# Ten of the modulation's tiles in attention instead of twelve, and begun 75 ticks after its start instead of 10

## The chip, the cores and the metric

The kernel runs on one core of a Trainium2 chip. The metric is the device time of one execution in microseconds, lower is better; it is given as the median over several executions. The engines are named as the profile names them: PE is TensorE (matmuls; PEld its weight loads), DVE is VectorE, ACT is ScalarE, POOL is GpSimd, and SP is SyncE, which here mostly issues DMAs.

## The reference

A step of a small diffusion backbone with two layers, width 1024, for 512 latent tokens and 128 context tokens. The first layer's mixer is a bidirectional scan (SSD), the second's is differential attention with 8 heads; each is followed by a gated convolutional network (ConvGLU) with a hidden width of 2816. Every sub-layer is normalised, shifted and scaled, and added back with a gate; shift, scale and gate come from a modulation of the conditioning vectors.

```python
def modulation(cvec, w, b):
    m = jax.nn.silu(cvec) @ w + b          # w: 1024 x 6144 for each layer
    return jnp.split(m[:, None, :], 6, axis=-1)
...
    def one_block(qi):                     # differential attention, 128 queries at a time
        s = jnp.einsum('bqhcd,bkhcd->bhcqk', qi, k, preferred_element_type=F32) * DA_SCALE
        p = jax.nn.softmax(s, axis=-1)
        w = p[:, :, 0] - lam * p[:, :, 1]
        return jnp.einsum('bhqk,bkhd->bqhd', w.astype(v.dtype), v)
...
    for i in range(DEPTH):
        p_sh1, p_sc1, p_g1, p_sh2, p_sc2, p_g2 = modulation(c_ctx[None], mod_w[i], mod_b[i])
        s_sh1, s_sc1, s_g1, s_sh2, s_sc2, s_g2 = modulation(c, mod_w[i], mod_b[i])
        ...
        xp = xp + p_g1 * op
        xs = xs + s_g1 * os_
        xp = xp + p_g2 * conv_ffn(modulate(xp, norm_ffn_g[i], p_sh2, p_sc2), *ffn_p)
        xs = xs + s_g2 * conv_ffn(modulate(xs, norm_ffn_g[i], s_sh2, s_sc2), *ffn_p)
```

The change concerns `modulation` of the second layer: 6144 outputs for two conditioning vectors, each output a dot product over 1024 numbers.

## The kernel before

All activations lie transposed, 128 channels on the partitions and 640 tokens (512 latent, 128 context) in the free dimension; the width of 1024 is eight such tiles. A matrix product in fp32 is made of three matmuls of a split into a rounded high part and a rest (`whi`, `wlo` for weights, `h10h`, `h10l` and the like for activations), so each weight tile is loaded by SP (`raw`, or `raw_15523` with its running number), rounded on ACT (`whi<-raw`) and subtracted on DVE (`wlo<-raw,whi`). The stages follow each other: SSD, the first network (ffn0), attention, the second network (ffn1).

*The modulation of layer 1* is done on DVE, beside other stages. `mod_rest` goes over tiles t0 to t1 − 1 of 48. A tile `mw` is 128 outputs by 1024 weights, 512 KB, loaded by SP (L683) into one of two buffers, one tile ahead. For each of the two conditioning vectors `cb[c]` one DVE instruction multiplies and sums it (L690; the profile calls it CUSTOM_DVE_ANT_0, the order below ISA) into a column of `mod`. The first writes its products into a scratch tile `junk`, the second over `mw`, so that the buffer is free after it; each is followed by a short read of the accumulator. These are "the dots": two for each tile. After eight tiles the bias is added (`mod<-mod,modb`).

*What sets the order.* Side work is written as generators. `self.add(gen, wait)` starts one after `wait` ticks; a tick is a call of `hook()`, which the matrix products make once for each step over k. A `yield n` lets n ticks pass, and in attention `self.gap` is 6, so a tile of two dots takes 12 ticks. `self.drain(t)` runs the rest of a generator at once. Every dot is also held behind the matmul that was recorded last (`self.hold`). A scheduler then makes one fixed order for each engine from what was recorded, and moves other instructions around.

*Which tiles go where* stands in `DOTS`: tiles 0 to 3 at the end of SSD, then up to `DOTS[1]` in ffn0 (beside its up projections and its four calls of `project_out`, the down projection of a part of the hidden channels), the next up to `DOTS[2]` in ffn0's `project_last`, the next up to `DOTS[3]` in attention, and the last eight in ffn1.

*Attention.* `heads` records eight heads in a loop. A head has three dense products from the queue of `next_tile` (q, k, v; 24 ticks together, but none in head 0, whose products are done ahead by `start_tiles`), the rotation of q and k on DVE (`ru`, `q`, `k`, `rope`), and `att_head`: for each of four blocks of 128 queries two score tiles `sl` (one for each map; `sp` for the context's own), their maximum over the row on DVE (L1351, `sm<-sl`), the exponential on ACT (`e<-sl`, L103), the difference of the two maps on DVE (`w<-e,sm,e`), its transposition on PE (`wt`) with copies `wTh` on ACT and `wTl` on DVE, and the product with v (`ov`). The tail of a head normalises its output (`ms` on PE, the `rs_` steps on DVE, and a broadcast: by DMAs to `rsd` and back into `rbc` for heads 0 to 6, by PE into `obc` for head 7). `vout` and `kout` are outputs, `k<-in_ck` the cached keys.

After the loop come the splits of the first six heads' outputs (`o0` to `o5`), the rest of the dots (`self.drain(dots)`), the closing of the pool that holds `mw` (`self.modctx.close()`), and `self.restore()`, which loads the eight tiles of the residual stream `xr_15354` to `xr_15361` from DRAM (L139) into the space of that pool. Then the output projection of the first six heads is recorded (`project_out`, `po<-o0h,whi` and so on, with `xr<-po,mod,xr` on DVE as the gated addition), with head 7 still unfinished, and at last that of heads 6 and 7.

Of the kernel before, what the change touches and what calls it, by code (L numbers as in the profile page):

```python
# [40 lines left out]
RAW = 4  # L41
NS = 4
S0 = 5
DOTS = 4, 24, 28, 40, 48
TH = T // 2
ATT_SPLIT = 6
NF = 11
# [3 lines left out]
class Step:  # L51
# [659 lines left out]
    def ffn(self, l, h, nextnorm, pool):  # L711
# [151 lines left out]
        with self.tc.tile_pool(name=f"sums{l}", bufs=1, side="right", reuse_waits="tile") as tp:  # L863
            self.seven = self.add(operands(sevens, tp), 1)
            for s, (k0, k1) in enumerate(SUB):
                while done < min(k1 + 1, FT):
                    if done == (S0 + 1 if l else 3):
                        junk = lambda: self.slot("sq", "junk", BF16, cols=1024, bufs=1)
                        self.modtask = self.add(self.mod_rest(1, *(DOTS[3:] if l else DOTS[:2]),
                                                              self.cb, self.mod_row, junk), 1)  # L870
# [35 lines left out]
        if not l:  # L906
            self.gap = 3
            junk = lambda: self.slot("t", "junk", BF16, cols=1024, bufs=4)
            more = [self.add(self.mod_rest(1, *DOTS[1:3], self.cb, self.mod_row, junk), 1)]
        self.project_last(mid, range(*SUB[-1]), self.gate(l, 1), nextnorm, parts="CD" if l else "AB", save=not l,  # L910
# [95 lines left out]
    def ssd_group(self, g, xf, Bf, Cf, pool):  # L1006
# [51 lines left out]
        def state(d_, c, pm):  # L1058

            xw = sl("xw", "xw", 512, 2)  # L1060
            self.tt(v3(xw), v3(xt[:, c, :]), self.wst[:, c, heads(d_)].unsqueeze(2).to_broadcast([P, 8, 64]), ALU.mult)
            self.mm(pm, bt[:, c, :], xw, True, True)

        def carry(d_, c, out, pm):

            nh = sl("hs", f"h_{d_}_{c}_", 512, 6)
            if c == NL:
                self.act(nh, pm, AF.Copy)
                nc.sync.dma_start(a["st"][d_, g], nh)
                return  # L1070
            self.tt(v3(nh), v3(hs[d_, c]), self.cd[:, c, heads(d_)].unsqueeze(2).to_broadcast([P, 8, 64]), ALU.mult)
            self.tt(nh, nh, pm, ALU.add)
            hs[d_, out] = nh
# [107 lines left out]
    def ssd(self, h, dtps, nextnorm, pool):  # L1181
# [62 lines left out]
        self.gap, self.rest = 3, 2  # L1244
        early = self.add(self.mod_rest(1, 0, DOTS[0], self.cond_rows(row), row, junk), 4)
        self.project_last(hy, range(8), self.gate(0, 0), nextnorm, save=True, before=[early])
# [201 lines left out]
    def heads(self, h, nextnorm, pool):  # L1448

        nc = self.nc  # L1450
        self.cv = pool.tile([P, D], F32, tag="cv", name="cv", bufs=1)
        nc.sync.dma_start(self.cv, self.a["cv"])
        consts = self.att_consts(pool)
        next(consts)
        o, tk, self.tails, self.held = [], [], {}, {}
        next(consts, None)
        junk = lambda: pool.tile([P, 1024], BF16, tag="junk", name="junk", bufs=1)
        self.gap, self.rest = 6, 0
        dots = self.add(self.mod_rest(1, *DOTS[2:4], self.cb, self.mod_row, junk), 10)
        for hd in range(8):  # L1460
            q, qp = self.att_evac(self.next_tile(h, "q"), hd, "q", pool)
            k, kp = self.att_evac(self.next_tile(h, "k"), hd, "k", pool)
            nc.sync.dma_start(self.a["kout"][hd], kp)
            q = self.att_q(q, hd, pool)
            k = self.att_k(k, hd, pool)
            vs = []
            tk.append(self.add(self.att_head(hd, qp, kp, q, k, vs, o, pool), 1 if hd == 7 else 4))
            self.add(self.att_v(self.next_tile(h, "v"), hd, vs, pool), 1)
            if hd:
                self.drain(tk[hd - 1])  # L1470
        n0 = ATT_SPLIT
        for i in range(n0):
            self.drain(self.tails[i])
        hy = [self.split(o[i], f"o{i}") for i in range(n0)]
        self.drain(dots)
        self.modctx.close()
        self.restore()
        self.project_out(hy, range(n0), self.gate(1, 0), range(KT - 3))
        self.drain(tk[7])
        for t in self.tails.values():  # L1480
            self.drain(t)
        hy += [self.split(o[i], f"o{i}") for i in range(n0, 8)]
        self.project_last(hy, range(n0, 8), self.gate(1, 0), nextnorm, range(8), save=True)
# [200 lines left out]
```

## Time and profile before

| what | value |
|---|---|
| runs of the kernel | 1827.41, 1826.96, 1824.88 us |
| median | 1826.96 us |
| profiled execution, device time | 1828.54 us |
| its span from the first to the last instruction | 1826.8 us, mean PE clock 0.994 |
| ffn0's fourth `project_out` | about 869 to 897 us |
| the heads, from the rows of PE | about 1025 to 1330 us |
| first and last dot in attention | 1044.93 and 1259.49 us |

The profile is one execution. Starts are microseconds from the start of the span. A row of a timeline gives start, duration, engine, line and operation, `out<-in`, and in brackets how long the engine had been idle and what released it. A row of stretches gives window, length, busy time and instructions of PE, PEld, DVE, ACT and POOL, then the clock granted to PE (1.00 is full), the mean busy share of the DMA engines and GB/s. In the rows of one engine alone, only that engine's columns stand.

### The profile page before, as it was taken

Reading aid. Unit: us, or ns where it says so; the run is one execution under the profiler, and the core shown is the slowest. Engines: PE = TensorE matmul, PEld = TensorE weight load, DVE = VectorE, ACT = ScalarE, POOL = GpSimd, SP = SyncE. Lnnn points to the kernel's source line nnn. Section 1 sums busy time; section 2 is a strip of 40 time slices with the busy share of each in tenths; the row PEclk is TensorE's granted clock in tenths of the full one; section 3 lists DMA queues with packets and bytes.
Section 4 is the critical chain, followed back from the end, with each engine's and each line's share of the span. In section 5 each row is a group of like instructions: output and inputs, shape, how many; then the busy total and the mean of one; then the engine's idle time right before and its main releaser. Section 6 shows DMA issues by size and latency. Waiting matters only on the chain.

```text
span 1826.8 us, 33717 instructions
## 1 busy us (share of the span) xinstructions
PE 1778.1 (97%) x12914; PEld 1681.8 (92%) x12914; DVE 1480.0 (81%) x2947; ACT 1148.2 (63%) x2281; POOL 136.5 (7%) x164
## 2 busy tenths in 40 slices
PE   7999999999999999999999999999999999999996
PEld 5899999999989999999999988888889999999996
DVE  5789999999967968879588888888877677867686
ACT  3479686879525667667673555666647566656661
POOL 0000000000000021221210000000001012121210
PEclk9999999999999999999999999999999999999998
DMA  9744344446574596977776222223137457786881
GB/s 340 258 144 135 102 128 126 116 135 197 198 229 134 124 226 164 223 186 200 189 176 235 93 76 93 85 83 107 44 122 201 118 141 191 176 190 156 174 233 59
DMA packets 115613, 288.07 MB, mean 158 GB/s; under 512 B 13326, under 2 KB 20090, under 8 KB 115452
## 3 DMA queue, kind: packets, MB, share of 16 engines
q1 hardware_dynamic: 92348, 227.59, 37.9%
q0 software_dynamic: 22528, 57.81, 17.9%
q8 instruction: 101, 1.65, 0.4%
q10 hardware_dynamic: 576, 0.52, 0.1%
q14 instruction: 60, 0.49, 0.1%
HBM read 239.93 MB, written 34.80 MB: 150 GB/s over the span
## 4 chain that ended last, share of the span: by engine, by line
PE 87%; DVE 7%; ACT 3%; DMA 1%; issue 1%; SPq 0%; DVEq 0%; ACTq 0%; POOLq 0%
PE up L112 27%; PE po L112 25%; PE z L112 6%; PE x L112 5%; PE st L112 5%; PE bc L112 3%; PE yp L112 3%; PE k L112 2%; PE modrow L112 1%; PE q L112 1%; PE ov L112 1%; PE sl L112 1%; PE in L112 1%; ACT whi L103 1%; ACT e L103 1%
## 5 line engine op out<-in xcount | busy, mean ns | idle before, releaser
L103 ACT ACTIVATE whi<-raw 128x1024 fp32r<-128x1024 f32 (+2 forms) x259 | 225.4, 872 | 189.8 <-PE po L112 87.4
L109 DVE TENSOR_TENSOR wlo<-raw,whi 128x1024 fp32r<-128x1024 f32 (+2 forms) x196 | 193.3, 992 | 66.7 <-ACT whi L103 66.1
L112 PE MATMUL po<-mh,whi 128*128 128x256 f32 (+1 forms) x704 | 166.2, 309 | 0.7 <-ACT y L103 0.5
L112 PE MATMUL po<-ml,whi 128*128 128x256 f32 (+1 forms) x704 | 165.7, 309 | 0.2 <-DMA ml<-cv 0.2
L112 PE MATMUL po<-mh,wlo 128*128 128x256 f32 (+1 forms) x704 | 165.5, 308 | 0.0
L205 POOL DMA_DIRECT2D wlo<-in_w_up x62 | 53.9, 871 | 1256.1 <-ACT wlo L103 643.6
L109 DVE TENSOR_TENSOR wlo<-s,whi 128x512 fp32r<-128x512 f32 x136 | 91.3, 687 | 54.2 <-ACT whi L103 53.5
L112 PEld LDWEIGHTS po<-mh,whi 128*128 128x128 f32 x704 | 127.6, 188 | 1.8 <-ACT y L103 1.0
L112 PEld LDWEIGHTS po<-ml,whi 128*128 128x128 f32 x704 | 127.8, 188 | 0.5 <-DMA ml<-cv 0.5
L112 PEld LDWEIGHTS po<-mh,wlo 128*128 128x128 f32 x704 | 128.0, 188 | 0.0
L112 PE MATMUL up<-Th,whi 128*128 128x320 f32 x408 | 126.3, 310 | 0.2 <-ACT uraw L103 0.2
L112 PE MATMUL up<-Th,wlo 128*128 128x320 f32 x408 | 126.2, 309 | 0.0
L112 PE MATMUL up<-Tl,whi 128*128 128x320 f32 x408 | 126.1, 309 | 0.0
L112 PE MATMUL up<-h11h,wlo 128*128 128x320 f32 (+2 forms) x384 | 109.4, 308 | 0.0
L112 PE MATMUL up<-h01h,wlo 128*128 128x320 f32 (+2 forms) x384 | 109.4, 308 | 0.0
L112 PE MATMUL up<-h11l,whi 128*128 128x320 f32 (+2 forms) x384 | 109.4, 308 | 0.0
L112 PE MATMUL up<-h01h,whi 128*128 128x320 f32 (+2 forms) x384 | 109.4, 308 | 0.0
L112 PE MATMUL up<-h01l,whi 128*128 128x320 f32 (+2 forms) x384 | 109.4, 308 | 0.0
L112 PE MATMUL up<-h11h,whi 128*128 128x320 f32 (+2 forms) x384 | 109.3, 308 | 0.0
L103 ACT ACTIVATE whi<-s 128x512 fp32r<-128x512 f32 x136 | 83.2, 628 | 40.4 <-DVE s L109 34.4
L106 DVE SCALAR_TENSOR_TENSOR ca<-uraw,fcw,ca 128x511 f32<-128x511 f32 (+1 forms) x176 | 86.3, 546 | 12.1 <-ACT ca L103 10.5
L106 DVE SCALAR_TENSOR_TENSOR cv<-uraw,fcw,cv 128x511 f32<-128x511 f32 (+1 forms) x176 | 85.8, 546 | 5.6 <-ACT cv L103 5.4
(532 smaller groups left out, 5360.1 us busy)
## 6 DMA issues: line engine op xcount, KB each, us to landing
raw<-in_w_up SPq DMA_DIRECT2D x88, 512.0 KB, 4.8
mw<-in_modT SPq DMA_DIRECT2D x44, 512.0 KB, 4.3
raw<-in_w_in SPq DMA_DIRECT2D x40, 512.0 KB, 6.0
rb<-rowd SPq DMA_DIRECT2D x40, 512.0 KB, 5.2
wlo<-in_w_up POOLq DMA_DIRECT2D x36, 512.0 KB, 5.6
raw<-in_w_dn SPq DMA_DIRECT2D x64, 256.0 KB, 3.0
raw<-in_w_qkv SPq DMA_DIRECT2D x24, 512.0 KB, 3.5
mr<-in_mod SPq DMA_DIRECT2D x44, 256.0 KB, 6.0
```

The costliest lines, as they stand in the source:

```text
L103: return self.nc.scalar.activation(out, in_, func, **k)
L106: return self.nc.vector.scalar_tensor_tensor(out, in0, s, in1, op0, op1)
L109: return self.nc.vector.tensor_tensor(out, a, b, op)
L112: self.last = self.nc.tensor.matmul(out, lhsT, rhs, start=start, stop=stop, skip_group_check=more)
L205: self.nc.gpsimd.dma_start(lo[:, c], self.units[u][0][:, c], accum_op=ALU.add)
```

## The change

```diff
-DOTS = 4, 24, 28, 40, 48
+DOTS = 4, 26, 30, 40, 48
...
-        dots = self.add(self.mod_rest(1, *DOTS[2:4], self.cb, self.mod_row, junk), 10)
+        dots = self.add(self.mod_rest(1, *DOTS[2:4], self.cb, self.mod_row, junk), 75)
```

ffn0 does 22 tiles up to the end of its fourth `project_out` instead of 20, still four in `project_last` (26 to 29 instead of 24 to 27), and attention ten (30 to 39) instead of twelve. In attention the generator starts 75 ticks after its creation instead of 10. Head 0 finds its products done, and each later head brings 24 ticks, so it starts with head 4 (counted from 0) instead of head 1; on DVE the first dot now stands between the rotations of q of heads 3 and 4. With 12 ticks a tile, seven of the ten tiles fit into the remaining ticks, and `self.drain(dots)` records the others after the loop. ffn1 and SSD keep their order on every engine.

DVE in attention's second head, the row maxima of two scores, before (L1316 is part of the rotation of k, L1359 the reciprocal of the row sums):

```order
L109 TENSOR_TENSOR q<-q,ru 128x512
L1359 RECIPROCAL sm<-sm 128x2
L109 TENSOR_TENSOR sm<-sm,nlam 128x1
L106 SCALAR_TENSOR_TENSOR ql_12521<-q,qh_12520 128x512
L690 ISA junk,mod_116<-mw,cb 128x1024
L690 ISA mod_116 128x1
L1351 TENSOR_REDUCE sm<-sl 128x1 x2
L106 SCALAR_TENSOR_TENSOR w_12444<-e_12424,sm,e_12427 128x640
L109 TENSOR_TENSOR wlo_12662<-raw_12397,whi_12661 128x1024
```

And after:

```order
L109 TENSOR_TENSOR q<-q,ru 128x512
L1359 RECIPROCAL sm<-sm 128x2
L109 TENSOR_TENSOR sm<-sm,nlam 128x1
L106 SCALAR_TENSOR_TENSOR ql_12525<-q,qh_12524 128x512
L106 SCALAR_TENSOR_TENSOR w_12452<-e_12434,sm,e_12437 128x640
L1351 TENSOR_REDUCE sm<-sl 128x1 x2
L109 TENSOR_TENSOR wlo_12665<-raw_12407,whi_12664 128x1024
```

The dot in front of the two maxima is gone, and the `w` of the block before has moved to its place.

DVE at the end of attention, head 7's row maxima up to the first gated addition, before:

```order
L106 SCALAR_TENSOR_TENSOR w_15435<-e_15398,sm,e_15401 128x640
L109 TENSOR_TENSOR vl_15407<-vt,vh_15406 128x512
L1351 TENSOR_REDUCE sm<-sl 128x1 x2
L109 TENSOR_TENSOR wTl<-wt,wTh 128x512
L106 SCALAR_TENSOR_TENSOR xr_15354<-po,mod_116,xr_15354 128x256 x2
```

And after:

```order
L1351 TENSOR_REDUCE sm<-sl 128x1 x2
L690 ISA mw,mod_116<-mw,cb 128x1024
L690 ISA mod_116 128x1
L690 ISA junk,mod_116<-mw,cb 128x1024
L690 ISA mod_116 128x1
L1359 RECIPROCAL sm<-sm 128x2
L109 TENSOR_TENSOR vl_15407<-vt,vh_15406 128x512
L1351 TENSOR_REDUCE sm<-sl 128x1
L690 ISA mw,mod_116<-mw,cb 128x1024
L690 ISA mod_116 128x1
L109 TENSOR_TENSOR mod_116<-mod_116,modb 128x8
```

Before, no dot stands here; after, three of the last five do, and the other two stand a few rows ahead of these. The first gated addition into `xr_15354` comes 14 rows behind the last dot.

SP at the end of attention after the change, the loads of `xr` and what is around them:

```order
L166 DMA raw_15652<-in_w_ao 128x4x256
L1463 DMA out_kout<-kp_15134 128x128
L279 DMA rsd<-rs_y 4x160
L281 DMA rbc<-rsd 128x640
L683 DMA mw<-in_modT 128x1024
L139 DMA xr_15354<-xd_6149 128x640
L139 DMA xr_15355<-xd_6150 128x640
```

Before, the loads of `xr` stood ahead of `raw_15523`, `raw_15652` and head 7's `kout`. Now they stand behind these and behind the load of the last tile of `mw`.

## The prediction

> **What bounds the kernel now.** I read the page first: its busy shares, then the chain of work that ended last.
>
> ```profile
> PE 1778.1 (97%) x12914; PEld 1681.8 (92%) x12914; DVE 1480.0 (81%) x2947; ACT 1148.2 (63%) x2281; POOL 136.5 (7%) x164
> PE 87%; DVE 7%; ACT 3%; DMA 1%; issue 1%; SPq 0%; DVEq 0%; ACTq 0%; POOLq 0%
> ```
>
> TensorE holds 87% of the chain, VectorE 7%. A change that leaves the matmuls alone, as this one does, can win only what PE waits for. The dots of the modulation are on VectorE, so next I asked for everything that touches `mw`, which gives their price, and then for busy times in stretches: two stages of ffn0's down projection, two stretches of the early heads, and the one in which the heads end.
>
> ```profile
> L690 DVE CUSTOM_DVE_ANT_0 junk<-mw,cb x44: 1202/1221/1226, 620.7 to 1620.1; 128x1024 bf16<-128x1024 f32 x44
> DMA to landing us min/median/max: 3.1/4.3/6.6
> ```
> ```profile
> 712.00:740.00 28.00, 28.00 (x193) 28.00 (x193) 19.42 (x33) 15.40 (x34) 6.89 (x8) 1.00 0.88 236
> 869.00:897.00 28.00, 28.00 (x196) 28.00 (x195) 13.97 (x25) 17.02 (x36) 7.78 (x9) 1.00 0.85 202
> 1050.00:1100.00 50.00, 44.63 (x312) 39.35 (x310) 41.17 (x82) 28.81 (x64) 0.00 (x0) 0.97 0.25 80
> 1100.00:1150.00 50.00, 48.28 (x343) 42.87 (x343) 44.10 (x94) 30.96 (x66) 0.00 (x0) 1.00 0.26 84
> 1250.00:1305.00 55.00, 52.89 (x368) 44.91 (x365) 49.70 (x102) 37.56 (x78) 0.00 (x0) 1.00 0.30 100
> ```
>
> The first column after the length is PE, the third VectorE. A dot takes 1.22 us. In the down projection PE is full while VectorE idles 8.6 to 14 us of 28. In the heads both are near their limit: PE lacks 5.4 us of 50 in the first stretch, 1.7 in the next, and VectorE has only 5 to 9 us idle. What PE waits for there stands in the waits of PE from 1025 to 1310 us (total, times, longest):
>
> ```profile
> PE q L112 <- ACT e L103: 5.6, 6, 2.3
> PE v L112 <- ACT e L103: 3.0, 6, 1.0
> PE wpt L1400 <- DVE rs_v L242: 2.2, 5, 0.4
> PE wt L1417 <- DVE wTl L109: 1.7, 5, 0.4
> PE sl L112 <- ACT e L103: 1.2, 1, 1.2
> ```
>
> These are 13.7 us for all heads, and the longest ones lie between 1047 and 1101, in the second and third head; there PE's timeline has (start, duration, and the wait in front):
>
> ```profile
> 1047.87 0.56 PE L112 MATMUL v<-h10h,whi 128*128 128x256 f32 x2 [0.99 <-ACT e L103]
> 1058.48 0.57 PE L112 MATMUL sl<-kh,qh 64*128 64x320 f32 x4 [1.20 <-ACT e L103]
> 1061.90 0.56 PE L112 MATMUL q<-h10h,whi 128*128 128x256 f32 x2 [2.27 <-ACT e L103]
> 1063.23 0.73 PE L112 MATMUL q<-h10h,whi 128*128 128x256 f32 x2
> 1076.86 0.65 PE L1417 MATMUL wt<-cst,w 128*128 128x128 f32 x4 [0.34 <-DVE wTl L109]
> 1100.09 0.56 PE L112 MATMUL q<-h10h,whi 128*128 128x256 f32 x2 [1.52 <-ACT e L103]
> ```
>
> A score's bank comes free when `e` (the exponential on ACT) has read it; `e` waits for the row maximum on VectorE, and there a dot stands ahead of it. Three rows of VectorE, and two from the end of the same head, where the dot again stands ahead of a maximum and a cast on ACT ahead of `e`:
>
> ```profile
> 1044.93 1.22 DVE L690 CUSTOM_DVE_ANT_0 junk<-mw,cb 128x1024 bf16<-128x1024 f32 x1
> 1046.08 1.55 DVE L1351 TENSOR_REDUCE sm<-sl 128x1 f32<-128x640 f32 x2
> 1047.54 0.88 DVE L106 SCALAR_TENSOR_TENSOR w<-e,sm,e 128x640 f32<-128x640 f32 x1
> 1096.03 1.22 DVE L690 CUSTOM_DVE_ANT_0 mw<-mw,cb 128x1024 f32<-128x1024 f32 x1
> 1098.21 1.06 ACT L103 ACTIVATE whi<-raw 128x1024 fp32r<-128x1024 f32 x1 [2.96 <-PE v L112]
> ```
>
> The pair of 0.73 us behind the wait of 2.27 us, against 0.56 for the pair ahead of it, shows a slower clock. PE alone in short stretches (busy, clock):
>
> ```profile
> 1062.00:1064.00 2.00, 2.00 (x10) 0.61 0.01 2
> 1064.00:1066.00 2.00, 2.00 (x9) 0.53 0.00 0
> 1370.00:1372.00 2.00, 2.00 (x16) 0.50 0.92 321
> 1006.00:1009.00 3.00, 3.00 (x30) 1.00 1.08 335
> ```
> ```profile
> 1005.53 0.37 PE L112 MATMUL ms<-sq,cst 128*32 128x96 f32 x8 [2.31 <-ACT sq L103]
> 1369.77 0.55 PE L112 MATMUL ms<-sq,cst 128*32 128x96 f32 x8 [1.98 <-ACT sq L103]
> ```
>
> So a wait of 1.98 us was followed by half the clock, one of 2.31 us was not, and PE's row of 1100 to 1150 above, which opens with the wait of 1.52, reads a clock of 1.00. Four microseconds at a mean of 0.57 lose 4 x 0.43 = 1.7 us. [...]
>
> **The change part by part.** The sum is made against the profiled execution, 1828.54 us, and is then carried to the median of the runs, 1826.96 us, which is 1.58 lower; differences of a few microseconds carry over unchanged.
>
> *Two tiles go to ffn0.* Four dots, 4 x 1.22 = 4.9 us, land in the fourth project_out; the stretch 869 to 897 has 28 − 13.97 = 14 us of idle VectorE beside a full PE. Two loads of 512 KB join SP there, with DMA at 0.85, against 0.88 at 712. Cost: 0, since the stage at 712 keeps PE full with 5.4 us more of VectorE than this one; without that cover it would be the 4.9. The four dots of project_last keep their place and only change tiles.
>
> *Twelve dots leave heads 1 to 3* (counted from 0), 14.6 us of VectorE. Wait by wait: the 0.99 before `v` shrinks little, because a `w` of 0.88 us takes the dot's place ahead of the reduces: 1.22 − 0.88, about 0.3 gained (0 to 0.99). The 1.20 before `sl` stays (0 to 1.20 gained): ahead of its `e` stands a cast on ACT that waits for PE, as the one of 1098.21 did for 2.96 us. The 2.27 before `q` loses one dot outright, 1.22, and part of what a second one pushed back: 1.8 (1.2 to 2.27). The 0.34 goes (0 to 0.34). The 1.52 loses the dot of 1096.03, and ACT's cast of 1.06 us now stands behind `e`: 1.2 (1.1 to 1.52). Smaller ones to 1130, all waits on a `wTl`, `rs_v` or `e` that queues behind a dot:
>
> ```profile
> 1113.78 0.66 PE L1417 MATMUL wt<-cst,w 128*128 128x128 f32 x4 [0.17 <-DVE wTl L109]
> 1126.55 0.33 PE L1400 MATMUL wpt<-cst,wp 128*128 128x128 f32 x1 [0.45 <-DVE rs_v L242]
> 1127.32 0.56 PE L112 MATMUL v<-h10h,whi 128*128 128x256 f32 x2 [0.44 <-ACT e L103]
> ```
>
> give 0.8 (0.5 to 1.06); from the next head on the same two of 0.45 and 0.44 return each head with or without a dot, so nothing more is counted. Together 0.3 + 1.8 + 0.3 + 1.2 + 0.8 = 4.4 us (2.8 to 7.4). With 0.5 left of the 2.27 the nearest row is the 1.52 without a drop, so I take the slow clock as gone as well: 1.7, in all 6.1. What is late next is the wait of 1.20, and behind it PE's own work.
>
> *Heads 4 to 6* keep a dot every six ticks, as before: 0.
>
> *The end.* Only 7 of the ten tiles fit into the ticks that are left; the others are recorded when the loop over heads is over, where `drain(dots)` stands. Nine or ten dots lie where two lay: 8 more, 9.8 us of VectorE. It has 5.3 us idle from 1250 to 1305. The last five stand between the row maxima of head 7, and all the loads of `xr` wait for the last one, since they go into the space of `mw`. These rows carry the end before:
>
> ```profile
> 1259.49 1.23 DVE L690 CUSTOM_DVE_ANT_0 mw<-mw,cb 128x1024 f32<-128x1024 f32 x1 [0.79 <-PE q L112]
> 1303.69 1.55 DVE L1351 TENSOR_REDUCE sm<-sl 128x1 f32<-128x640 f32 x2
> 1307.60 0.89 DVE L106 SCALAR_TENSOR_TENSOR w<-e,sm,e 128x640 f32<-128x640 f32 x1 [1.01 <-ACT e L103]
> 1309.72 0.48 DVE L106 SCALAR_TENSOR_TENSOR xr<-po,mod,xr 128x256 f32<-128x256 f32 x1 [0.15 <-PE po L112]
> 1317.71 0.69 DVE L109 TENSOR_TENSOR wTl<-wt,wTh 128x512 fp32r<-128x512 f32 x1 [1.38 <-ACT wTh L103]
> 1328.46 1.35 PE L112 MATMUL obc<-rs_y,cst 128*128 128x160 f32 x8 [1.51 <-DVE rs_y L106]
> ```
>
> 9.8 us of dots less 5.3 of idle leave 4.5. The row of 1307.60 waited 1.01 for ACT, which is slack: 3.5 at that `w`, while the maxima of head 7's first blocks, which come before most of the dots, stay about on time. On the way from `w` to `obc` (transposes, `ov`, squares, `rs_y`) VectorE has one more such gap of 1.38: 2.1. So `obc` comes at +2.1 to +4.5; I take 2.8, the middle of 2.1 and 3.5. PE cannot put it off: it is idle before `obc` already. Below: 0, if more of the idle time takes dots. Above: the whole 9.8, and 1.7 of clock.
>
> The last dots have a DMA in front too. The last tile's load can go only when the tile two ahead is done, by my walk through the new order at about 1294.8; with 4.3 us (3.1 to 6.6) it lands at 1298 to 1301.5, and VectorE, which works in order, gets to its dot at about 1300. A stop of up to 1.5 us, in front of head 7's maxima and its `w`, is inside the 4.5. The last dot ends near 1304 and lets the `xr` loads go; priced like `mw`'s, they land at 1307 to 1311, against a first use at 1309.72.
>
> *Sum:* 0 − 6.1 + 2.8 = −3.3 us.
>
> **The rivals.**
>
> *The end pays in full (slower).* Place: VectorE from head 7's second block to the first update of `xr`. The three last pairs stop for `mw`'s last load, the maxima behind them stop `e`, and `e` holds the score banks, so PE stops too; the `xr` loads then land late and `po`'s banks are not read. For it: VectorE is at 49.70 of 55 us, and the last load has no margin. Against it: 5.3 us idle, and `po` work that PE has between the blocks. Price: all 9.8 us, and 1.7 of clock after a stop over 2 us, against 4.4 won in the heads with the slow clock left there: +7.1, about 1834.1; with 6.1 won, 1832.4. It decides where `obc` comes 8.0 us later: 8.0 − 4.4 = 3.6, 1830.6.
>
> *The end costs nothing.* The last `w` is hidden by PE's own rows, `obc` at +0 to +1: −5.1 to −6.1, about 1821.4. Against: `obc` is waited for today already.
>
> *A wash.* The heads give the 2.8 of the lower bounds and the clock dip stays, because 1.20 and what is left of the 2.27 fall close together; the end costs 2.8: 1827.0.
>
> *Nothing happens in the early heads,* since `e`, ACT's casts and PE gate each other and a dot fills time that nobody wants: gain 1, loss 2.8: 1828.8. The reduces that start the moment the dot ends speak against it.
>
> **How the numbers follow.** Forecast: 1826.96 − 3.3 = 1823.7, chance 0.42; with the heads at 4.4 to 6.1 and the end at 2.1 to 4.5 it runs from 1823.0 to 1827.1, and to 1820.0 with the heads' upper bound, the clock and an end at 2.1. End for nothing 0.20; wash or nothing early 0.13; paid in full 0.25. The range 1820.0 to 1832.4 leaves out more than 7.0 from heads and clock with an end for nothing, and the upper part of the slower rival. 0.2% is 3.65 us, about what a measurement of this kernel can tell: faster is below 1823.3, slower above 1830.6. Faster: the end for nothing and nearly half of the forecast, 0.40. Same: the rest of the forecast, the wash, and a little of the rival, 0.36. Slower: the rest of it, 0.24.
>
> **What would show it.** Right: in the heads to 1130 the 2.27 and 1.52 are gone or under 0.5, the stretch 1062 to 1066 reads a clock of 1.00, and head 4 starts 4 to 6 us sooner; ffn0 ends when it did; the wait before `obc` is 3 to 5 us. Wrong: the fourth project_out has waits of PE; `e` holds `q` as long as before; or PE's waits between 1285 and 1330 sum to 8 us more than before, with `mw` or `xr` loads as what VectorE waited for.

## The result: slower, and the profile after

| | before | after |
|---|---|---|
| median of six runs each | 1825.92 us | 1834.39 us |
| lowest and highest | 1824.09, 1830.37 | 1832.89, 1836.15 |
| profiled execution, its span | 1828.54, 1826.8 | 1833.84, 1832.0 |

The ratio is 1.0046 (95% interval 1.0035 to 1.0056): the change costs 8.5 us by the medians. The profiled executions differ by 5.3 only, because the one of before lies 2.6 us above its median and the one of after 0.6 below; where the one of before lost time shows below.

The page of after, its busy shares, shows that no engine got more instructions to do. PE is busy 3.9 us longer with the same 12914 matmuls, at a mean granted clock of 0.993 against 0.994:

```profile
PE 1782.0 (97%) x12914; PEld 1682.9 (92%) x12914; DVE 1480.6 (81%) x2947; ACT 1149.4 (63%) x2281; POOL 136.8 (7%) x164
```

To find the place I took rows of PE that stand in both traces: the first start tile of attention, then the transposition `wpt` once a head, `obc`, the last `ms` of the next normalisation, and `nbc` at the end of the program. Of before (1126.55, 1328.46 and 1369.77 stand in the prediction):

```profile
1005.84 0.39 PE L112 MATMUL st<-h10h,whi 128*128 128x256 f32 x1
1274.97 0.33 PE L1400 MATMUL wpt<-cst,wp 128*128 128x128 f32 x1 [0.45 <-DVE rs_v L242]
1814.19 1.09 PE L112 MATMUL nbc<-rs_y,cst 128*128 128x64 f32 x4 [2.49 <-DVE rs_y L106]
```

And of after:

```profile
1005.64 0.39 PE L112 MATMUL st<-h10h,whi 128*128 128x256 f32 x1
1124.73 0.33 PE L1400 MATMUL wpt<-cst,wp 128*128 128x128 f32 x1 [0.45 <-DVE rs_v L242]
1275.72 0.33 PE L1400 MATMUL wpt<-cst,wp 128*128 128x128 f32 x1 [0.45 <-DVE rs_v L242]
1333.33 2.50 PE L112 MATMUL obc<-rs_y,cst 128*128 128x160 f32 x8 [3.94 <-DVE rs_y L106]
1377.16 0.37 PE L112 MATMUL ms<-sq,cst 128*32 128x96 f32 x8 [1.98 <-ACT sq L103]
1819.73 1.62 PE L112 MATMUL nbc<-rs_y,cst 128*128 128x64 f32 x8 [2.48 <-DVE rs_y L106]
```

| stretch | before | after | difference |
|---|---|---|---|
| start tile to `wpt` of head 2 | 120.71 | 119.09 | −1.62 |
| to `wpt` of head 6 | 148.42 | 150.99 | +2.57 |
| to `obc` | 53.49 | 57.61 | +4.12 |
| to the last `ms` | 41.31 | 43.83 | +2.52 |
| to `nbc` | 444.42 | 442.57 | −1.85 |

The early heads gain 1.6, those from there to head 6 give back more than that, and the end loses 6.6 in two pieces. A trace is one execution, so I read the same stretches in the traces of the experiments below. From the start tile to `wpt` of head 2, the three other kernels begun at 75 ticks with the same gap (e1, e7, e8) take 119.14 to 121.17 us, and four that begin at 10 (e2, e9, e11, e12) 120.68 to 121.91: the early gain is about 1 us, and the traces scatter by as much. The second row is firmer: the same three take 149.85 to 150.43, and six with the dots in the places of before (e2, e3, e5, e9, e10, e12) 148.39 to 148.84. The last line is chance: before, the clock fell behind the `ms` at 1369.77 (0.50 in the prediction's rows), which the later part of that trace pays, and after, behind the `ms` at 1377.16, it did not (1.00 from 1377 to 1380); e12, whose PE keeps the order of before, takes 442.35 there.

The loss before `obc` is in the chain of waits after, from 1293.7 to 1305.7 us (start, length, what; a piece of a chain is shorter than the instruction where the next starts early). The first line is its share by line:

```profile
by line: DVE mw L690 28.2%; DVE sm L1351 25.9%; DVE junk L690 18.9%; DVE o5l L109 6.2%; issue 5.6%; DVE wTl L109 5.0%; DVE vl L109 4.9%; PE sl L112 4.8%; ACT e L103 2.5%; DVE mod L109 0.8%; DVE sm L1359 0.7%; DVE mod L690 0.3%; ACTq L103 0.
1293.76 0.82 DVE sm L1351
1294.58 1.13 DVE mw L690
...
1296.46 1.14 DVE junk L690
...
1299.67 1.13 DVE mw L690
...
1300.81 1.14 DVE junk L690
...
1303.46 1.13 DVE mw L690
```

All five dots are in the chain: 28.2% + 18.9% of 12.0 us, 5.7 us, beside row maxima that head 7's exponentials wait for. VectorE does not pause between them, from 1294.50 to 1304.59. Over the whole stretch from head 6's `wpt` to `obc` VectorE works 6.7 us more than before (51.38 us against 44.70) and idles 2.6 us less; the 4.12 is the difference.

The loss behind `obc` is PE's clock (busy, clock), against 1.00 in the same stretches before:

```profile
1332.00:1336.00 4.00, 2.67 (x10) 0.50 0.47 154
1336.00:1340.00 4.00, 4.00 (x21) 0.65 0.00 0
```

2.67 x 0.50 + 4.00 x 0.35 = 2.7 us, the +2.52 of the table. The slow clock at 1062 stayed as well:

```profile
1062.00:1064.00 2.00, 2.00 (x10) 0.58 0.00 0
1064.00:1066.00 2.00, 2.00 (x13) 0.57 0.00 0
```

### The profile page after: what moved, and what is told of

The parts are those of the page before. It is cut to its first block, busy times and chain, and to the rows that moved or that the text cites. A ratio compares the mean times of both kernels' runs of the same rounds, so it can differ in the third digit from the quotient of the medians.

```text
span 1832.0 us, 33724 instructions
## 1 busy us (share of the span) xinstructions
PE 1782.0 (97%) x12914; PEld 1682.9 (92%) x12914; DVE 1480.6 (81%) x2947; ACT 1149.4 (63%) x2281; POOL 136.8 (7%) x164
## 5 line engine op out<-in xcount | busy, mean ns | idle before, releaser
L106 DVE SCALAR_TENSOR_TENSOR ca<-uraw,fcw,ca 128x511 f32<-128x511 f32 (+1 forms) x176 | 86.2, 545 | 12.0 <-ACT ca L103 10.4
```

Source lines behind the costliest of these rows:

```text
L106: return self.nc.vector.scalar_tensor_tensor(out, in0, s, in1, op0, op1)
```

## The experiments

Each kernel is the one before with the edit shown, unless said otherwise, and each ratio is against runs of the kernel before on the same chip.

| label | median, us | before, us | ratio (95% interval) |
|---|---|---|---|
| e1_late_twelve | 1835.99 | 1825.56 | 1.0057 (1.0043 to 1.0071) |
| e2_early_ten | 1826.78 | 1825.56 | 1.0008 (0.9999 to 1.0017) |
| e3_wait34_ten | 1826.26 | 1825.56 | 1.0001 (0.9992 to 1.0010) |
| e4_no_dots | 1844.48 | 1825.56 | 1.0100 (1.0086 to 1.0114) |
| e9_five_more | 1832.48 | 1826.22 | 1.0041 (1.0026 to 1.0055) |
| e7_late_seven | 1835.04 | 1826.22 | 1.0048 (1.0035 to 1.0061) |
| e5_wait70_ten | 1835.19 | 1826.22 | 1.0047 (1.0034 to 1.0060) |
| e6_late_dense | 1826.21 | 1826.22 | 0.9997 (0.9988 to 1.0006) |
| e8_filler | 1830.41 | 1826.64 | 1.0020 (1.0011 to 1.0029) |
| e11_five_mid | 1829.94 | 1826.64 | 1.0020 (1.0011 to 1.0030) |
| e10_wait58_eight | 1829.74 | 1826.64 | 1.0014 (1.0005 to 1.0022) |
| e12_extra_load | 1825.63 | 1826.91 | 0.9993 (0.9984 to 1.0002) |

**The two edits apart.** `wait` stands for the last argument of `self.add` in `heads`.

```diff
e1: DOTS = 4, 24, 28, 40, 48    wait 10 -> 75
e2: DOTS = 4, 26, 30, 40, 48    wait 10
```

> Only the late start (75 ticks), with the twelve tiles of before; nine dots instead of five are recorded after the loop over heads. If the end is what costs (dots between head 7's maxima and the residual loads), four more dots there, 4.9 us of VectorE, make it slower than the changed kernel: +11 to +14 us against before, with a wait before obc of 7 us or more. If the dots' new places in heads 4 to 6 cost, it is as the changed kernel, +8. If the two tiles in ffn0 cost, it is close to before.

> Only the two tiles moved to ffn0, with the old start at 10 ticks; the last dot comes a head sooner. If the end or the places of the dots cost, this is free: 0 to -1 us against before, ffn0 ends when it did. If ffn0's fourth down projection pays for four dots, +2 to +5 us.

The late start alone costs 10.4 us, below the 11 to 14 expected; the two tiles in ffn0 cost nothing that these runs can tell (+1.2, interval across 1). So it is the late start. The wait of 7 us in front of `obc` did not come in one piece: in e1 PE stops there for 3.24 us, and at two earlier places for 1.99 and 1.88. That the loss grows with each dot left over is not shown: nine dots go with +10.4, five with +8.5, the four of e5 below with +9.0, and the intervals overlap.

**Late, but with nothing left after the loop.** e3 begins 24 ticks later than before; e6 begins at 75 ticks as the change does, and puts the dots closer.

```diff
e3: DOTS = 4, 26, 30, 40, 48    wait 10 -> 34
e6: DOTS = 4, 26, 30, 40, 48    wait 10 -> 75    self.gap 6 -> 4
```

> The ten tiles begun after 34 ticks: head 1 is free of dots, the dots of the others have the places of before, and all are recorded by the end of the loop over heads, with no dot behind the last q. If the end costs, the whole loss of 8 us is gone and head 1's waits are the gain: -1 to -3 us against before. If a late start costs by itself, +3 or more.

> The changed kernel with 4 ticks between dots instead of 6: the late start stays, six dots go in a head instead of four, and none is left after the loop. If the bunch is the loss, most of the 8 us is gone: -1 to +3 us against before, the rest being what two more dots a head cost. If the heads from the fourth on cannot take dots at all, +6 or more.

Both are as fast as before. In e6 no dot is left, and PE's waits from 1280 to 1340 us are again those of before:

```profile
PE obc L112 <- DVE rs_y L106: 1.5, 1, 1.5
PE po L112 <- ACT e L103: 1.0, 2, 0.7
```

So a late start need not cost; what it leaves for after the loop does, and, less, the places of its dots in the heads, of which more below. The gain expected of e3 did not show in its median.

**The bunch alone.** Nothing is moved, and five dots into a spare tile are recorded where the change leaves its five (e9), or behind the tasks of head 3 (e11).

```diff
         self.drain(dots)
+        w = self.mod_row()
+        nc.sync.dma_start(w, self.a["modT"][39])
+        spare = pool.tile([P, 8], F32, tag="spare", name="spare", bufs=1)
+        for j in range(5):
+            self.hold(nc.vector.tensor_tensor_reduce(junk(), w, self.cb[0], 1.0, 0.0, ALU.mult, ALU.add,
+                                                     spare[:, j:j + 1]), [self.last])
         self.modctx.close()
```

> The kernel before, with nothing moved, plus five extra dots (their results go to a spare tile) recorded after the loop over heads, where the changed kernel records its last five; the residual loads wait for the last one. If these five are the loss, obc comes 3 to 5 us later and PE's clock drops behind the longer wait: +4 to +8 us against before. If the loss is made in heads 3 to 6 by where the dots stand, 0 to +1.

> The kernel before with the same five extra dots as in the run with five more at the end, but recorded behind the fourth head's tasks, within 17 rows of VectorE. If it is the place at the end that makes dots dear (no matmuls but the scores' own to go on with, and the chain to obc behind), these cost little: +0 to +2 us. If any bunch of five stops the softmax and PE, +5 to +6 as at the end.

At the end they cost 6.3 us (4.7 to 10 by the interval's ends). The wait before `obc` and the clock behind it, as in the change:

```profile
1330.81 1.44 PE L112 MATMUL obc<-rs_y,cst 128*128 128x160 f32 x4 [3.22 <-DVE rs_y L106]
```
```profile
1330.00:1334.00 4.00, 3.19 (x12) 0.57 0.46 154
1334.00:1338.00 4.00, 4.00 (x30) 1.00 0.00 0
```

In the middle they cost 3.3 (2.0 to 5.5 by the interval's ends), more than the 0 to 2 expected. VectorE is full for 20 us, and PE pays behind it with waits and clock (columns as in the stretches of the prediction):

```profile
1140.00:1150.00 10.00, 9.89 (x69) 8.92 (x68) 10.00 (x20) 4.98 (x13) 0.00 (x0) 1.00 0.17 55
1150.00:1160.00 10.00, 8.90 (x56) 6.69 (x55) 9.90 (x17) 5.09 (x8) 0.00 (x0) 1.00 0.24 66
1160.00:1170.00 10.00, 8.10 (x37) 7.01 (x37) 6.33 (x13) 5.77 (x13) 0.00 (x0) 0.66 0.33 111
```

So this bunch in a softmax stops PE as well. That the end makes a bunch dearer is not shown: the two intervals overlap, and in the traces the stretch around the bunch is longer by 7.1 us in e11 (`wpt` of head 2 to that of head 4, 80.22 against 73.10) and by 5.5 in e9 (`wpt` of head 6 to the last `ms`, 100.29 against 94.80). The extra tile of e11 also holds one of the two `mw` buffers, which shifts other dots, so neither figure is the price of five dots alone.

**The clock.** The changed kernel, with small matmuls in the wait before `obc`, released by the first step of the `rs_` chain (`self.rsv`):

```diff
+            def filled():
+                bc = self.wide("obc")
+                for _ in range(12):
+                    self.hold(self.mm(bc[:, :160], self.ident, self.cst[:, :160], True, True), [self.rsv])
+                return bc
-            bc = yield from self.rms_bcast(lambda: self.wide("obc"), [sq], 0, T, P, 4)
+            bc = yield from self.rms_bcast(filled, [sq], 0, T, P, 4)
```

> The changed kernel with twelve small matmuls (ident by cst, into the bank of obc, overwritten by it) on PE between the start of the last rs_ chain and obc, about 3 us of work in the wait of 3.94. If the clock's drop behind that wait is part of the loss, the stretch after obc reads 1.00 instead of 0.50 and 0.65, and the time from obc to the end of the normalisation's sums falls by 2 to 2.5 us: +5 to +7 against before. If the drop does not hang on PE's idle time, the clock stays at 0.5 and the time at +8.

```profile
1330.00:1334.00 4.00, 4.00 (x30) 1.00 0.00 0
1334.00:1338.00 4.00, 3.59 (x26) 1.00 0.46 154
1338.00:1342.00 4.00, 4.00 (x29) 1.00 0.00 0
```

The clock stays at 1.00, and the loss falls from 8.5 to 3.8 us, by more than expected. So this drop hung on PE's idle time: with the wait of 3.94 us empty the clock read 0.50 and 0.65 behind it, with the wait filled 1.00. Not all of the 4.7 is the clock: seven matmuls of `po` also moved in front of the real `obc`, which fills some of the wait with useful work. The profiled execution, the slowest of eleven (1834.15), shows 2.2 of it: from head 7's `wpt` to the last `ms` 63.09 us, against 65.27 in the change and 62.86 before. Where the rest was won the trace does not show. The 36.17 us from head 6's `wpt` to head 7's stay, against 31.94 before; that part is the bunch itself.

**Fewer dots in the heads.**

```diff
e4: DOTS = 4, 36, 40, 40, 48    dots = None (no dots in attention)
e7: DOTS = 4, 29, 33, 40, 48    wait 10 -> 75
e10: DOTS = 4, 26, 32, 40, 48    wait 10 -> 58
```

> No dots in attention at all: twelve more tiles than before in ffn0 instead. It shows the most that taking dots out of the heads can bring. If a dot in a head delays PE by the waits behind it, the heads lose nearly all of q, wt and the slow clock after 1062 us: -4 to -8 us, as long as ffn0 hides its dots. If PE is paced there by e, casts and itself, -1 to -2 us. If ffn0 has no room, slower.

> The late start (75 ticks) with seven tiles in attention, three more in ffn0: the dots in the heads stand as in the changed kernel, and only one is left after the loop. If the bunch after the loop is the loss, it is gone: 0 to -2 us against before, with a wait before obc of about 1.5. If the places in heads 4 to 6 are the loss, the heads still lose 2 to 3 us and the time is +1 to +3.

> Eight tiles in attention begun after 58 ticks (four whole tiles behind the start of before, so the dots keep their places in the heads), none left after the loop; project_last of ffn0 does six tiles instead of four. If place and bunch are all that costs, heads 1 and 2 are free and nothing is lost: -1 to -3 us against before. If project_last has no room for four more dots, attention starts later by as much and it is 0 to +4.

All three are slower. In e7 and e4 most of the time goes ahead of attention, whose start tile comes at 1012.53 and 1015.32, against 1005.84 before: ffn0 has no room for what they send there. In e7 two waits of PE appear behind the fourth project_out, where the change has none:

```profile
900.68 0.63 PE L112 MATMUL up<-Th,whi 128*128 128x320 f32 x1 [2.38 <-ACT uraw L103]
967.89 0.56 PE L112 MATMUL po<-ml,whi 128*128 128x256 f32 x2 [3.52 <-DMA ml<-cv]
```

In e10, which sends four more dots to `project_last` and loses 3.1 us, the wait for `sq` in front of attention is 4.74 instead of 2.31. Their heads tell more. In e7 the end is that of before: 1.51 in front of `obc`, and 53.45 us from head 6's `wpt` to it, against 53.49. In e4, with no dot in any head, a head is no shorter than before with its four dots: 36.97 us from head 3's `wpt` to head 4's, against 36.59 (1163.06 to 1199.65):

```profile
1177.85 0.33 PE L1400 MATMUL wpt<-cst,wp 128*128 128x128 f32 x1 [0.45 <-DVE rs_v L242]
1214.82 0.33 PE L1400 MATMUL wpt<-cst,wp 128*128 128x128 f32 x1 [0.45 <-DVE rs_v L242]
```

Dots in their old places cost such a head nothing that the traces can tell; a head with them takes 36.46 to 37.10 in the traces of e2, e3, e9, e10 and e12.

**The dots' places in the later heads.** Between the `wpt` of heads 3 and 6 VectorE in the change waits, once a head, in front of the normalisation of the head before, which holds up the copy `vl` that PE waits for. The first of the three:

```profile
1179.22 0.88 DVE L106 SCALAR_TENSOR_TENSOR o<-o,sg,rbc 128x640 f32<-128x640 f32 x1 [0.82 <-DMA rbc<-rsd]
1180.76 0.33 PE L1417 MATMUL wt<-cst,w 128*128 128x128 f32 x1 [0.62 <-DVE vl L109]
```

SP issued `rbc` and, right behind it, a load of `mw`; before, that load went ahead of `rbc` by 4.6 us. After:

```profile
1174.64 0.38 SPq L281 DMA_DIRECT2D rbc<-rsd  x1
1175.43 0.33 SPq L683 DMA_DIRECT2D mw<-in_modT  x1
```

and before:

```profile
1171.53 0.33 SPq L683 DMA_DIRECT2D mw<-in_modT  x1
1176.11 0.38 SPq L281 DMA_DIRECT2D rbc<-rsd  x1
```

The start moved by 65 ticks, which is not a multiple of a tile's 12, so every load took another place in its head. e5 moves it by 60; e12 leaves all as before and puts a load behind `rbc`.

```diff
e5: DOTS = 4, 26, 30, 40, 48    wait 10 -> 70
e12:
         self.nc.sync.dma_start(bc, d.partition_broadcast(P))
+        if self.extra in (2, 3, 4, 5):        # the number of the head
+            x = pool.tile([P, 640], F32, tag="extra", name="extra", bufs=1)
+            self.hold(self.nc.sync.dma_start(x, self.a["modT"][39][:, :640]), [first])   # first: the DMA to rsd
```

> Ten tiles begun after 70 ticks, five whole tiles behind the start of before, so that each dot has the place within its head that it has before; four dots are left after the loop instead of five. If the place costs the 0.4 to 0.6 us a head, heads 4 to 6 go back to 36.6 us each, and the end still loses about 4 of 5 of its loss: +4 to +6 us. If a later start alone makes those heads longer, they keep 37.1 and it is +6 to +8.

> The kernel before, every engine's order of PE, VectorE and ACT unchanged, with an extra load of 128x640 (320 KB, into a spare tile) issued by SP right behind rbc in four heads, where the changed kernel issues mw. If it is the load of mw behind rbc that makes PE wait for vl in the changed kernel's heads 4 to 6, VectorE waits for rbc in these heads (some 0.5 to 0.8 us), PE's wait at wt for vl comes up at 0.3 to 0.6 us a head, and it is +1 to +2.5 us against before. If the dots' own places make that wait, nothing of it shows: 0.

e5 gives the heads back: 36.51 and 36.48 us from the `wpt` of head 3 to that of head 4 and on to head 5's, against 37.23 and 37.10 in the change, and no wait for `rbc`:

```profile
1162.88 0.33 PE L1400 MATMUL wpt<-cst,wp 128*128 128x128 f32 x1 [0.45 <-DVE rs_v L242]
1199.39 0.33 PE L1400 MATMUL wpt<-cst,wp 128*128 128x128 f32 x1 [0.45 <-DVE rs_v L242]
1235.87 0.33 PE L1400 MATMUL wpt<-cst,wp 128*128 128x128 f32 x1 [0.45 <-DVE rs_v L242]
```
```profile
1179.61 0.88 DVE L106 SCALAR_TENSOR_TENSOR o<-o,sg,rbc 128x640 f32<-128x640 f32 x1
```

Its time does not follow: four dots are left after the loop, and in their order PE stops for 2.39 us at a `po` before `obc` too, with a clock of 0.50 from 1299 to 1305 behind it. From head 6's `wpt` to `obc` it takes 61.80 us, against 57.61 in the change, so its end loses what its heads win. In e12 VectorE waits for `rbc` in two of the four heads, but only 0.30 and 0.25 us, PE waits for no `vl`, and the time is that of before:

```profile
1178.99 0.89 DVE L107 SCALAR_TENSOR_TENSOR o<-o,sg,rbc 128x640 f32<-128x640 f32 x1 [0.30 <-DMA rbc<-rsd]
```
```profile
1174.93 0.38 SPq L282 DMA_DIRECT2D rbc<-rsd  x1
```

In the change's first two heads SP issues its next load 1.24 and 2.86 us behind `rbc`, and VectorE waits for `rbc` too, so its time can be read there:

```profile
1104.82 0.88 DVE L106 SCALAR_TENSOR_TENSOR o<-o,sg,rbc 128x640 f32<-128x640 f32 x1 [0.26 <-DMA rbc<-rsd]
1137.83 0.89 DVE L106 SCALAR_TENSOR_TENSOR o<-o,sg,rbc 128x640 f32<-128x640 f32 x1 [0.36 <-DMA rbc<-rsd]
```

Issued at 1101.28 and 1134.37, it took 3.54 and 3.46 us to VectorE's start. With 512 KB of `mw` issued 0.79 us behind it in the later heads it took 4.46 to 4.58; with 320 KB issued 0.43 or 0.44 us behind it in e12, 4.06, 4.02 and in a third head at most 3.68. How a load issued later slows one issued before it is not shown. That the places cost is shown by e5, and by the 149.85 us and more of the kernels that share the change's places. That the load behind `rbc` is the whole of it is not: the three waits for `vl` make 1.7 of the 2.57, and e12 reproduced none of them.

## Why the prediction was wrong

Forecast was −3.3 us; up to the last `ms` the traces differ by +7.6. Of the 10.9 between them the early heads make 4.5 (−6.1 forecast, −1.6 measured), the later heads 2.6 (0 forecast), the clock behind `obc` 2.5 (0 in the sum), and the way to `obc` 1.3 (2.8 forecast, 4.1 measured).

- **The end, which was mis-sized.** The prediction counted eight more dots, 9.8 us, against VectorE's 5.3 us of idle time and the gaps of 1.01 and 1.38, and took 2.8. Only six dots came behind head 6's `wpt`, 6.7 us of work, and idle time took up only 2.6 of it. The five last met none: the chain holds them one after the other, 5.7 us. The +4.12 is near the upper bound of the step, 4.5. Idle time counts only where it lies beside the work that is added.
- **The clock at the end.** The prediction forecast a wait of 3 to 5 us before `obc`, and it was 3.94, but its sum counted no clock for it (only the upper bound and the rival did), though its own rows had a drop behind 1.98 (0.50) and 2.27 (0.61 and 0.53). It lost 2.5. This term was put at nothing without a reason. The end with its clock is 4.1 + 2.5 = 6.6, and e9, which adds a bunch of five alone, made +6.3.
- **The heads to 1130.** The single waits fell where a dot stood ahead of `e`, most of them by less than was walked: in order 0.99, 1.20, 2.27, 0.34, 1.52 became

```profile
1047.42 0.39 PE L112 MATMUL v<-h10h,whi 128*128 128x256 f32 x1 [0.76 <-ACT e L103]
1058.04 0.56 PE L112 MATMUL sl<-kh,qh 64*128 64x320 f32 x4 [1.20 <-ACT e L103]
1061.01 0.38 PE L112 MATMUL q<-h10h,whi 128*128 128x256 f32 x1 [1.83 <-ACT e L103]
1076.15 0.66 PE L1417 MATMUL wt<-cst,w 128*128 128x128 f32 x4 [0.21 <-DVE wTl L109]
1097.98 0.38 PE L112 MATMUL q<-h10h,whi 128*128 128x256 f32 x1 [0.24 <-ACT e L103]
```

  The 1.52 and the 1.20 were right. The 2.27, for which 1.8 was taken, gave 0.44. The prediction credited a dot there that does not stand there: before, what delays the maximum that this `q` waits for is a `w`, and the last dot ends 3 us ahead of that.

```profile
1054.81 1.22 DVE L690 CUSTOM_DVE_ANT_0 mw<-mw,cb 128x1024 f32<-128x1024 f32 x1
1059.26 0.88 DVE L106 SCALAR_TENSOR_TENSOR w<-e,sm,e 128x640 f32<-128x640 f32 x1
1060.12 1.54 DVE L1351 TENSOR_REDUCE sm<-sl 128x1 f32<-128x640 f32 x2
```

  After, the maximum starts at 1059.22, as soon as PE has done the scores (1058.72 + 0.46), and the wait is still 1.83: it is the maximum and the exponential themselves. The clock fell behind it as behind the 2.27 (0.58 and 0.57), so the 1.7 that hung on it was not won. Of the smaller waits, taken at 0.8, the 0.45 in front of `wpt` is there again. Of the 6.1 came 1.6.
- **Heads 4 to 6 at 0** was wrong, within the +2.57: the dots keep their distance, but they and their loads do not keep their place in the head.
- **ffn0 at 0** was right: e2 cannot tell it from nothing, and the fourth projection had no wait of PE. In e7, with three tiles more, the cover has ended.
- The rival that the end pays in full, at 1832.4 to 1834.1, came nearest to 1834.39, in part by luck. Its mechanism was partly there: maxima behind dots, a long stop of PE (3.94 us), and a slow clock behind it (0.50 and 0.65). But the dots did not stop for `mw`'s last load (VectorE has no gap up to 1304.59), and the additions into `xr` did not wait for their loads (the first starts at 1309.41 with no wait, the later ones wait for `po` alone). Its sizes were off both ways: it priced the end at 9.8 + 1.7 = 11.5 and the heads at −4.4 or −6.1, where the end cost 6.6 and all heads together +1.0.

## What to carry to other kernels

Side work that a generator spreads over a stage must end inside it: what a late start leaves over is drained in one piece, where nothing spreads it, and here that piece fell into the chain to the next stage (+4.1 us to `obc`, +2.5 of clock behind it). Idle time of an engine is a budget for added work only where the work is free to wait for it: here it took up 2.6 of 6.7 us. And loads and dots that keep their distance may still land in worse places: here a start shifted by whole periods of what it feeds (e5) kept the heads as they were (36.5 us a head), and one shifted by 65 ticks did not (37.1 and 37.2).

## What the hardware showed that was not expected

Between 1000 and 1400 us, PE's clock fell behind waits of 1.72 us (e11, 0.66 over 1160 to 1170), 1.83 (the change, 0.58 and 0.57), 1.98 (before, 0.50 and then 0.73), 2.27 (before, 0.61 and 0.53) and 2.39 (e5, 0.50), but not behind others of 1.98 (the change, at 1377.16, 1.00) and 2.31 (before, 1.00). Behind the waits before `obc` of 3.94 us (the change, 0.50 and 0.65) and 3.22 (e9, 0.57) it fell as well. The four of these drops that lie in the traces of before and after cost 1.5 to 2.7 us each, 0.7 to 0.9 of the wait ahead, so each of these waits was paid 1.7 to 1.9 times. In e8, matmuls that compute nothing of use, put into such a wait, kept the clock at 1.00.

The broadcast `rbc` took 3.5 us where SP issued its next load 1.24 us or more behind it, and 4.5 with a load of 512 KB issued 0.79 us behind it, although that load stands behind it in SP's queue. With 320 KB behind it (e12) the delay was 0.6 us at most.
